# RWKV's output products in two groups of one shape (state, then u) instead of by turns

## The chip, the cores and the metric

One core of a Trainium2 chip runs the kernel. The metric is the device time of one execution in microseconds (us), the median of several; lower is better. TensorE (PE) does the products, VectorE (DVE) and ScalarE (ACT) take results out of the accumulation banks, GpSimd (POOL) works on SBUF alone, SyncE (SP) issues most DMAs.

## The reference

The reference is the trunk of a diffusion model: two layers over 256 context tokens and 256 latent tokens of 1024 features. Each layer has a token mixer of two halves of 512 features, RWKV-7 (eight heads of 64) and gated linear attention (GLA), then a feed-forward block (dense in layer 0, top-2 of 8 experts in layer 1). Both mixers run forwards and backwards over the tokens. The part that matters here is RWKV's recurrence:

```python
def step(s, inp):
    r_t, w_t, k_t, v_t, kk_t, a_t = inp
    s = (s * w_t[:, :, None, :]
         - jnp.einsum('bhvk,bhk->bhv', s, kk_t)[..., None] * (kk_t * a_t)[:, :, None, :]
         + v_t[..., None] * k_t[:, :, None, :])
    return s, jnp.einsum('bhvk,bhk->bhv', s, r_t)
```

Only the latent tokens' output is returned, so layer 1 needs RWKV's outputs of the context tokens only as a state.

## The kernel before, in words

**Chunks.** The recurrence is worked out in chunks of 64 tokens. A batch b (0 to 7) is one step of the chunked recurrence, for all eight heads and both directions at once: batches 0 to 3 are the context tokens, 4 to 7 the latent ones. Within a batch there are 8 places (d, p): direction d and pair of heads p. The even head of a pair lies on partitions 0 to 63 (`lo`), the odd one on 64 to 127 (`hi`).

**Lanes.** A batch passes through these generators: `rwkv_front` (lane F, L710) makes decays and scaled vectors; `rwkv_pairs` (P, L794) the triangular products between tokens, and sends the matrices that are to be inverted to DRAM (L820, L821); `rwkv_invert` (I, L837) loads their diagonal blocks back (L843) and inverts them on POOL (L848, L849); `rwkv_load` (L, L855) sends the result to DRAM (L862) and loads it as the tile Q (L864); `rwkv_mid` (M, L868) begins with DVE's transpose of Q into R (L896) and doubles the size of the blocks by products on PE (L884, L885); `rwkv_chain` (C, L946) does the recurrence: products with the old state (L961, L962), with the inverse (L970, L971), for the new state (L979, L980), and then the outputs y (L996 to L1012). `rwkv_post` (Z) and `rwkv_bonus` (B) finish the tokens; `ada` (A, L388) is independent work on the next modulation weights, put between as filler.

**Order.** The order in which the lanes take their steps is a string written out by hand for each layer, `RW_ORDER` (L52), played by `play` (L214). A step is what a generator does between two `yield`s. `may` (L1260) holds a step back only by counts of finished batches and steps. Each engine runs its instructions in the order in which they were issued, so the string fixes the order on every queue.

**The outputs.** For each place (d, p) the output is the sum of two products: the triangular matrix with u and the values (L1000: the weights u are 128 partitions by 64 columns, so all rows and half of the columns of the array), and the scaled vectors with the old state S (L1002: 64 partitions by 64 columns). The results of the even heads go to partitions 0 to 63 of one accumulation bank `a`, those of the odd heads to partitions 64 to 127 of another, `b_`. Float32 operands make two instructions of each product in the trace. One step does direction 0 (16 products, 32 instructions), the next direction 1, and the step after takes the sums out of both banks (L1005 to L1010). With S None (batch 0 of layer 0; layer 1's batch 0 makes no y) there is no product with the state. Layer 0 makes y for all eight batches, layer 1 for batches 4 to 7: 12 batches in all, 11 of them with both kinds of product.

Of the kernel before, what the change touches and what calls it, by code (L numbers as in the profile page):

```python
# [16 lines left out]
P = 128  # L17
# [14 lines left out]
# blocks of 128 columns of w_in in the order of use: rw r 0-3, k 4-7, v 8-11, w 12, a 13, g 14;  # L32
# gla q 0-1, k 2-3, v 4-7, o 8-11, a 12
ORDER = ([("gl", b) for b in (12, 2, 0, 4, 5, 3, 1, 6, 7, 8, 9, 10, 11)] +
         [("rw", b) for b in (14, 12, 13, 8, 9, 10, 11, 4, 0, 5, 1, 6, 2, 7, 3)])
# blocks after which the columns of GLA's q, k, v of a pair of heads, of its gate, and of RWKV's v are there
GLA_QKV, GLA_O, GLA_V = (5, 9), 13, 20
FGROUPS = [(0, 8), (8, 15), (15, 22)]
# weight pieces before the second layer's w_in
FFN_END = 24 + 8 + 14 + 4 + 22 + 24  # L40
SCRATCH = {"ogs": (P, 4, T), "vfirst": (P, 4, T), "rx": (P, 8, 256), "nsc": (2, 64, 1024), "tsc": (2, 64, 1024)}
# the order in which the lanes of a layer's projections with GLA, and of its RWKV, take their steps
# [23 lines left out]
# columns of the per-layer vectors  # L66
# [8 lines left out]
# columns of the per-layer small matrices  # L75
# [6 lines left out]
# columns of the constants  # L82
# [9 lines left out]
def constants():  # L92
# [7 lines left out]
    s = q % C  # L100
# [5 lines left out]
    # alpha comes at half its size  # L106
# [10 lines left out]
    # rows of the odd, and of the even, blocks of 16 of either half  # L117
# [5 lines left out]
def body(tc, nc, A):  # L123
# [19 lines left out]
    def banks(**bufs):  # L143
        """The eight banks divided anew."""
        if psum[0] is not None:
            psum[2].close()
        psum[2:] = [ExitStack()]
        psum[0] = psum[2].enter_context(tc.tile_pool(name=nm("pp"), bufs=1, space=PSUM))
        psum[1] = bufs
# [32 lines left out]
    def bc(ap, n):  # L182
        """[P, ..., a] seen as [P, ..., a, n]."""
        return bass.AP(tensor=ap.tensor, offset=ap.offset, ap=[*ap.ap, [0, n]])

    def bcm(ap, n):
        """[P, ...] seen as [P, n, ...]."""
        a = ap.ap
        return bass.AP(tensor=ap.tensor, offset=ap.offset, ap=[a[0], [0, n], *a[1:]])
# [5 lines left out]
    def steps(g, n):  # L195
        """n steps of g; whether it goes on."""
        for _ in range(n):
            if next(g, g) is g:
                return False
        return True  # L200
# [5 lines left out]
    def interleave(*gens, fill=None, rate=1):  # L206
        """A step of each in turn until all are through, and rate steps of fill beside them."""
# [6 lines left out]
    def play(lanes, order, may, extra={}):  # L214
        """Steps of the lanes (lists of generators, one after the other) in a given order; may(lane, done, step) tells
        whether a lane's next step may come. What is passed over or left is made in the end.
        extra: what a letter does that is no lane's."""
# [21 lines left out]
    # ------------------------------------------------------------ weight stream  # L239
    pieces = []  # L240

    class Stream:
# [23 lines left out]
        def room(self, n):  # L266
            """The pieces that there is room for when the first n are through."""
            return n + NR + (self.nx if self.more is not None else 0)

        def widen(self, p, n):  # L270
            """n more places for pieces, of pool p."""
# [4 lines left out]
        def split(self, upto):  # L276
            """Half pieces up to upto as two float32r parts."""
# [14 lines left out]
        def ahead(self, k, n):  # L292
            """Split half piece k and those up to n - 1 after it, as far as they are of a kind."""
# [16 lines left out]
        def half(self):  # L310
            """The next half piece; the one after it is split too, and more where there is room."""
# [3 lines left out]
        def get(self):  # L315
            """The next piece, both halves; the one after it is split too where there is room."""
# [26 lines left out]
    # the experts' chunks of 256 columns: 0, 1 the halves of gate and up, 2 down, which runs behind  # L343
# [12 lines left out]
    def dense_gen(out, hl, off, stride, xh, xl, ks, n0, n1):  # L356
        """out[128 features, tokens n0..n1] over the blocks ks of 128, in three float32r passes."""
# [11 lines left out]
    def dense_steps(out, w, xh, xl, n0, each):  # L369
        """out[128 features, tokens n0..] with one half piece, three products and a step at a time."""  # L370
# [8 lines left out]
    # ------------------------------------------------------------ modulation  # L379
# [8 lines left out]
    def ada(l, i0, i1, tag="acc"):  # L388
        """Columns 256 * i0.. of silu(c) @ ada_w + ada_b, features on partitions."""
# [29 lines left out]
    def staggered(gens, lag):  # L419
        """Each generator lag steps behind the one before."""  # L420
# [10 lines left out]
    class Squares:  # L431
        """Sums over the features of the squares of n columns."""
# [5 lines left out]
        def ready(self):  # L438
            """The table of Ln, before it is waited for."""
# [10 lines left out]
        def mm(self, keep=0):  # L450
            """The products of all but the last keep."""
# [4 lines left out]
        def r(self):  # L456
            """(mean + eps) ** -0.5, on all partitions."""
# [15 lines left out]
    def norm_mod(l, which, res, r, n0, hh, hl, tp, keep=None):  # L473
        """Modulation of res (tokens n0..) times r, as two float32r parts."""
# [20 lines left out]
        # every engine has a share  # L495
# [14 lines left out]
    def gated(l, which, dst, src, k, n0):  # L510
        """dst = src times the gate of feature block k, tokens n0.. (both hold these)."""
# [5 lines left out]
    def add_out(m, r, res, tp, nxt=None, dst=None):  # L517
        """dst = res + m r; the squares of the sums go to nxt."""
# [21 lines left out]
    # ------------------------------------------------------------ gated linear attention  # L540
    def gla_pair(l, n0, hp, M2, gab, q_, gk, gv, gad, og, tp, need):
        """Heads 2 hp and 2 hp + 1: their share of og becomes the mixer's output."""
# [81 lines left out]
        for n in range(0, 8, 2):  # L624
# [7 lines left out]
            # contributions to the state: chunks of even and odd place in different banks  # L632
# [53 lines left out]
    # ------------------------------------------------------------ RWKV-7  # L686
    # A batch b = 4 seg + i is the step i of a segment's recurrences: chunk i forwards, chunk 3 - i backwards, of all
    # eight heads. Tiles have [direction, pair of heads].
    NB = 16              # the blocks that are inverted row by row
# [3 lines left out]
    def image(t, b, q):  # L693
        """Block q of all matrices of batch b in DRAM: [head, direction, pair; NB rows; NB columns]."""
# [3 lines left out]
    def chunk(b, d):  # L698
        """The tokens of batch b in direction d."""
# [4 lines left out]
    def cut(t, b):  # L704
        """[.., tokens] as [direction, .., 64] of batch b."""
# [4 lines left out]
    def rwkv_front(l, b, X, tp):  # L710
        """Decays, and alpha, rho, beta, kappa scaled by them; the bonus."""
# [30 lines left out]
        # F: beta, kappa  # L742
# [36 lines left out]
    def rwkv_bonus(l, b, X, tp):  # L779
        """k_eff of both directions, r, r_k, summed over a head, times v."""  # L780
# [13 lines left out]
    def rwkv_pairs(l, b, X, tp):  # L794
        """The triangular products between tokens."""
        need_y = l == 0 or b >= 4
        arl, bk, Pt = X["scaled"].pop(b)
        # columns 0: with alpha, before t; 1: with rho, up to t. Rows of even heads: beta, kappa; of odd: kappa, beta
# [16 lines left out]
        # Nt: N transposed forwards, N backwards: above the diagonal either way  # L815
# [6 lines left out]
        # beta, kappa with tokens on partitions  # L822
# [14 lines left out]
    def rwkv_invert(b, X, tp):  # L837
        """A diagonal block to a lane: L = (I - N)^-1 forwards, its transpose backwards."""
# [16 lines left out]
    def rwkv_load(b, X, tp):  # L855
        """The inverted diagonal blocks come back."""
        # forwards (I - N)^-1 grows in Q and its transpose in R, backwards the other way round
# [10 lines left out]
    def rwkv_mid(l, b, X, tp):  # L868
        """(I - N)^-1 from its diagonal blocks, by doubling their size; values beside the places of u."""
# [4 lines left out]
        # values under (even heads) or over (odd) the places of u  # L874
# [17 lines left out]
        def alternate(x, d):       # the columns of every other block of 16  # L892
# [22 lines left out]
        # blocks of 16: their rows and columns lie by turns  # L915
# [20 lines left out]
        for d in range(2):  # L936
            # the transpose: above the diagonal forwards
# [8 lines left out]
    def rwkv_chain(l, b, X, tp):  # L946
        """A step of the recurrences, and its outputs."""
# [45 lines left out]
        if not need_y:  # L993
            yield True
            return
        a, b_ = ps("pc"), ps("pc")  # L996
        for d in range(2):
            for d_, p, o in mats[4 * d:4 * d + 4]:
                for t, h, u, A_ in ((a, lo, ux, AX), (b_, hi, uy, AY)):
                    mm(t[h, o], u[:, d, p, :], A_[:, d, p, 1, :], start=True, stop=S is None)  # L1000
                    if S is not None:
                        mm(t[h, o], S[h, d, p, :], arl[h, d, p, 1, :], start=False, stop=True)  # L1002
            yield
        y = cut(X["y"], b)
# [9 lines left out]
    def rwkv_post(l, b, X, tp):  # L1014
        """Head norm, bonus and gate of the tokens that are through with batch b."""
# [39 lines left out]
    def mixing(l, hctx):  # L1055
        """Token mixing of layer l; hands back its results (y of the heads, og) and their pools."""
# [47 lines left out]
        def conv_silu(pt, b, dst, s0):  # L1104
            """dst = 2 silu(conv(p)) over columns s0.."""
# [11 lines left out]
        def kk_norm(i):  # L1117
            """k k_k over its norm, halved."""
# [18 lines left out]
        def project(blocks):  # L1137
            """The blocks of h @ w_in that come next in the weight stream, a few products at a time."""
# [38 lines left out]
        def residual():  # L1177
            """v += (v of the first layer - v) * sigmoid(v0 + v @ v_down @ v_up)"""
# [43 lines left out]
        with pool("rw", "right") as tp:  # L1222
# [15 lines left out]
            def og_back():  # L1238
                """The other mixer's results come back, into the place of kk, which is through."""
# [20 lines left out]
            def may(n, done, step):  # L1260
                """What a step takes is there, and so is room for what it makes."""
# [21 lines left out]
            def warm(step):  # L1283
                """A product that nobody takes: the tensor engine's clock falls to half when it has had little to do."""
# [79 lines left out]
    def moe(l, res, r):  # L1364
# [12 lines left out]
        with pool("mh", "right") as hp:  # L1377
# [18 lines left out]
            # tokens on partitions  # L1396
# [10 lines left out]
            # the two greatest logits, the first of equals  # L1407
# [18 lines left out]
            # a token's place among those of its expert, and how many an expert has  # L1426
# [9 lines left out]
            # their weights  # L1436
# [23 lines left out]
        def choose(es, base, gt, g, w, tp, bufs):  # L1460
            """One-hot matrices of the slots base..base+127 of experts es: G tokens by slots, GT slots by tokens, w their
# [356 lines left out]
```

## Time and profile before

| what | value |
|---|---|
| time, median of 3 runs | 2515.29 us (2515.1 to 2521.45) |
| span of the profiled execution, first to last instruction | 2510.1 us |
| the median less that span | 5.2 us |
| PE busy | 2287.4 us, 91% of the span, 14765 matmuls |
| DVE busy | 1531.4 us, 61% |
| ACT busy | 1283.8 us, 51% |
| POOL busy | 248.0 us, 10% |
| mean granted TensorE clock | 0.917 |

The profiled execution's own time is not listed apart from its span; the 5.2 us between the median and the span are what lies around the instructions. The granted clock is 1.0 at 2.4 GHz and 0.5 at 1.2 GHz; a fraction between is a mean over a stretch. RWKV's stage of layer 0 runs from about 288 to 610 us of the span, that of layer 1 from about 1330 to 1605 us. A busy PE is not PE at its peak: matmuls overlap, so how fast products follow each other is read from their starts, not from their durations.

### The profile page before, as it was taken

To read this page: it belongs to the slowest core of one execution; us is meant where nothing else is said; L and a number is where in the kernel's file an instruction comes from. 1 tells how busy PE (TensorE), PEld (TensorE's weight loads), DVE (VectorE), ACT (ScalarE), POOL (GpSimd) and SP (SyncE) were. 2 spreads that over 40 slices of the span, in tenths; PEclk is the share of its full clock that TensorE was granted. 3 is DMA by queue.
4 is the path that set the end of the run, shared out by engine and by line. 5 is a ranking of instruction groups with operands and counts; after the bars stand their busy time and mean duration, and the time that the engine had idled before them with its cause. 6 is when DMAs were issued, how large, how long until landed. Compare 5 with 4: busy or idle time off the path is not lost. (4 is left out here: it accounts for less than half of the span.)

```text
span 2510.1 us, 37231 instructions
## 1 busy us (share of the span) xinstructions
PE 2287.4 (91%) x14765; PEld 1796.9 (72%) x14765; DVE 1531.4 (61%) x2236; ACT 1283.8 (51%) x1893; POOL 248.0 (10%) x597
## 2 busy tenths in 40 slices
PE   6999789998879999979997789869999999999997
PEld 3777577766658888847865667648787877877875
DVE  3647454623253233355674553358999898899996
ACT  3434443433342322354453442467777777777775
POOL 2000053320010000020002443000000000000000
PEclk8989888876979999988996988779999999999999
DMA  6211213452211313122222342248998998999992
GB/s 250 88 58 68 89 41 106 123 169 86 99 50 59 128 67 128 56 81 84 85 84 85 99 140 76 75 161 333 343 358 335 337 354 336 349 350 348 358 353 85
DMA packets 110310, 431.31 MB, mean 172 GB/s; under 512 B 51584, under 2 KB 54144, under 8 KB 61744
## 3 DMA queue, kind: packets, MB, share of 16 engines
q1 hardware_dynamic: 102800, 378.06, 41.9%
q10 hardware_dynamic: 5472, 39.85, 4.6%
q0 software_dynamic: 1856, 10.95, 1.2%
q8 instruction: 118, 1.93, 0.3%
q14 instruction: 64, 0.52, 0.1%
HBM read 418.33 MB, written 10.49 MB: 171 GB/s over the span
## 5 line engine op out<-in xcount | busy, mean ns | idle before, releaser
L289 DVE TENSOR_TENSOR lo<-raw,hi 128x1024 fp32r<-128x1024 f32 (+1 forms) x668 | 798.2, 1223 | 207.6 <-ACT hi L288 193.9
L288 ACT CAST hi<-raw 128x1024 fp32r<-128x1024 f32 (+1 forms) x668 | 685.2, 1048 | 156.0 <-PE ps_acc L1523 68.0
L1523 PE MATMUL ps_acc<-hi,gh 128*128 128x512 f32 x704 | 284.8, 405 | 0.0
L1523 PE MATMUL ps_acc<-hi,gl 128*128 128x512 f32 x704 | 278.3, 395 | 0.0
L1523 PE MATMUL ps_acc<-lo,gh 128*128 128x512 f32 x704 | 277.8, 395 | 0.0
L375 PE MATMUL ps_acc<-hh,hi 128*128 128x512 f32 (+1 forms) x448 | 180.5, 403 | 13.7 <-ACT hh L503 11.7
L375 PE MATMUL ps_acc<-hl,hi 128*128 128x512 f32 (+1 forms) x448 | 171.9, 384 | 2.9 <-POOL hl L507 2.1
L375 PE MATMUL ps_acc<-hh,lo 128*128 128x512 f32 (+1 forms) x448 | 171.5, 383 | 1.5 <-DVE lo L289 1.5
L1523 PEld LDWEIGHTS ps_acc<-lo,gh 128*128 128x128 f32 x704 | 132.1, 188 | 32.3 <-DVE lo L289 0.2
L1523 PEld LDWEIGHTS ps_acc<-hi,gl 128*128 128x128 f32 x704 | 132.4, 188 | 27.2
L1523 PEld LDWEIGHTS ps_acc<-hi,gh 128*128 128x128 f32 x704 | 132.2, 188 | 27.4
L1547 PE MATMUL ps_pc<-hi,eah 128*128 128x512 f32 x352 | 139.5, 396 | 0.0
L1547 PE MATMUL ps_pc<-lo,eah 128*128 128x512 f32 x352 | 139.0, 395 | 0.0
L1547 PE MATMUL ps_pc<-hi,eal 128*128 128x512 f32 x352 | 139.0, 395 | 0.0
L375 PEld LDWEIGHTS ps_acc<-hh,hi 128*128 128x128 f32 x448 | 88.4, 197 | 37.8 <-ACT hh L503 6.3
L375 PEld LDWEIGHTS ps_acc<-hl,hi 128*128 128x128 f32 x448 | 88.4, 197 | 19.8 <-POOL hl L507 3.6
L375 PEld LDWEIGHTS ps_acc<-hh,lo 128*128 128x128 f32 x448 | 88.3, 197 | 18.6 <-DVE lo L289 2.8
L1337 DVE TENSOR_TENSOR s<-s,ps_pa 128x512 f32<-128x512 f32 x22 | 15.1, 688 | 140.9 <-PE ps_pa L363 140.9
L848 POOL TENSOR_TENSOR Tt<-Nl,Tl 64x15 f32<-64x15 f32 (+7 forms) x240 | 71.9, 300 | 159.3 <-DMA Nl<-nsc 142.4
L396 PE MATMUL ps_acc<-raw,silc 128*32 128x256 f32 x768 | 66.2, 452 | 23.0 <-DMA raw<-ada 12.6
L533 POOL TENSOR_TENSOR xn<-macc,rstd 128x256 f32<-128x256 f32 x2 | 1.8, 925 | 842.7 <-ACT rstd L461 842.7
L453 PE MATMUL ps_pc<-nsq,ones 128*128 128x512 f32 (+1 forms) x112 | 57.3, 637 | 30.2 <-ACT nsq L447 30.1
(410 smaller groups left out, 4649.0 us busy)
## 6 DMA issues: line engine op xcount, KB each, us to landing
raw<-moe SPq DMA_DIRECT2D x264, 1024.0 KB, 6.1
raw<-ada ACTq DMA_DIRECT2D x34, 1024.0 KB, 5.3
raw<-win SPq DMA_DIRECT2D x28, 1024.0 KB, 4.9
raw<-fgu SPq DMA_DIRECT2D x22, 1024.0 KB, 4.8
raw<-ada SPq DMA_DIRECT2D x14, 1024.0 KB, 5.0
raw<-fdn SPq DMA_DIRECT2D x16, 448.0 KB, 3.2
res<-xc POOLq DMA_DIRECT2D x2, 2048.0 KB, 12.8
Q<-tsc SPq DMA_DIRECT2D x32, 128.0 KB, 2.8
```

The lines of the kernel that those rows point to most:

```text
L288: sc.copy(hi[:, :n], t[:, a * HALF:a * HALF + n])
L289: ve.tensor_tensor(lo[:, :n], t[:, a * HALF:a * HALF + n], hi[:, :n], ALU.subtract)
L375: mm(out, a[:, o], x[:, k, n0:T], start=(k == 0 and j == 0), stop=(k == KB - 1 and j == 2))
L396: mm(pt[32 * q:32 * q + 32, :256], silc[:, k, :], raw[:, k * 256:k * 256 + 256], start=(kk == 0), stop=(kk == 1), tile_position=(0, 32 * q))
L453: mm(self.pt, ones, self.todo.pop(0)[:, :self.n], start=(self.made == 0), stop=(self.made == KB - 1))
L533: e.tensor_tensor(t, m[:, k, :], r, ALU.mult)
L848: gp.tensor_tensor(tmp[:, u, j], bc(Nl[:, s, t], s + 1), bcm(Tl[:, s, j], NB - 1 - s), ALU.mult)
L1337: ve.tensor_tensor(s, s, pu, ALU.mult)
L1523: mm(pg, x[:, k, :], ww, start=(k == 0 and j == 0), stop=(k == 7 and j == 2))
L1547: mm(pd[q], x[:, i * P:i * P + P], ww, start=(c == 0 and i == 0 and j == 0), stop=(c == 10 and i == 1 and j == 2))
```

## The change

The 32 products of a batch's outputs are the same. They are issued as all 16 products with the state, a step boundary, all 16 products with u, a step boundary. The number of steps stays. The opening flag (`start`), which before stood on each product with u, stands on the first product in each bank alone; the products with u then add to what lies there. With S None the first of the two steps is empty, and the second has all 16 products with u. The rest of the diff takes comments away without moving a line; behind L1003 the lines move down by seven.

```diff
         a, b_ = ps("pc"), ps("pc")
-        for d in range(2):
-            for d_, p, o in mats[4 * d:4 * d + 4]:
-                for t, h, u, A_ in ((a, lo, ux, AX), (b_, hi, uy, AY)):
-                    mm(t[h, o], u[:, d, p, :], A_[:, d, p, 1, :], start=True, stop=S is None)
-                    if S is not None:
-                        mm(t[h, o], S[h, d, p, :], arl[h, d, p, 1, :], start=False, stop=True)
-            yield
+        if S is None:
+            yield
+        else:
+            for n, (d, p, o) in enumerate(mats):
+                for t, h in ((a, lo), (b_, hi)):
+                    mm(t[h, o], S[h, d, p, :], arl[h, d, p, 1, :], start=(n == 0), stop=False, skip_group_check=True)
+            yield
+        for n, (d, p, o) in enumerate(mats):
+            for t, h, u, A_ in ((a, lo, ux, AX), (b_, hi, uy, AY)):
+                mm(t[h, o], u[:, d, p, :], A_[:, d, p, 1, :], start=(S is None and n == 0), stop=True,
+                   skip_group_check=True)
+        yield
```

## Rows read from the trace of the kernel before

**Rows 1.** The page: busy time of all engines, and the clock in 40 slices.

```profile
PE 2287.4 (91%) x14765; PEld 1796.9 (72%) x14765; DVE 1531.4 (61%) x2236; ACT 1283.8 (51%) x1893; POOL 248.0 (10%) x597
...
PEclk8989888876979999988996988779999999999999
```

**Rows 2.** Busy time in a stretch of layer 0's RWKV: us, engines, clock, DMA share, GB/s.

```profile
400.00:450.00 50.00, 49.49 (x652) 36.95 (x652) 26.62 (x55) 22.00 (x47) 13.72 (x38) 0.87 0.30 86
```

**Rows 3.** PE's waits, 345 to 600 us: us in total, times, longest.

```profile
PE ps_pc L980 <- DVE uy L974: 2.9, 1, 2.9
...
PE ps_acc L404 <- ACT arow L400: 0.7, 2, 0.5
```

**Rows 4.** Lines 1000 and 1002: matmuls, ns min/median/max, first and last start, form.

```profile
L1000 PE MATMUL ps_pc<-AX,ux x192: 222/270/370, 358.1 to 1591.5; 128*64 128x64 f32 x192
...
L1002 PE MATMUL ps_pc<-arl,S x352: 218/267/367, 391.9 to 1592.8; 64*64 64x64 f32 x176
```

**Rows 5.** Timeline of PE in the first output step of batch 1, layer 0: start, us.

```profile
391.62 0.33 PE L1000 MATMUL ps_pc<-AX,ux 128*64 128x64 f32 x2
391.88 0.33 PE L1002 MATMUL ps_pc<-arl,S 64*64 64x64 f32 x2
```

**Rows 6.** The 17 stretches of output steps with both kinds: us, PE busy, clock, DMA.

```profile
391.62:395.73 4.11, 4.11 (x34) 0.99 0.16 34
396.74:403.19 6.45, 6.45 (x36) 0.50 0.30 104
424.39:428.49 4.10, 4.10 (x33) 1.00 0.25 43
429.97:434.52 4.55, 4.55 (x35) 0.86 0.70 236
...
535.06:539.22 4.16, 4.16 (x33) 0.98 0.82 321
541.09:547.31 6.22, 6.22 (x38) 0.50 0.07 8
...
1540.31:1549.59 9.28, 9.28 (x65) 0.81 0.22 54
...
sum 111.71, PE 111.71; mean PE 6.57
```

**Rows 7.** Groups of one shape: L970/L971; L1000 of batch 0; L884/L885. Columns of rows 2.

```profile
376.67:377.75 1.08, 1.08 (x34) 1.01 (x33) 0.00 (x0) 0.00 (x0) 0.00 (x0) 1.00 0.06 23
...
359.13:360.27 1.14, 1.14 (x30) 1.00 (x30) 1.13 (x2) 0.06 (x1) 0.98 (x3) 1.00 0.00 0
...
385.18:387.08 1.90, 1.90 (x33) 1.78 (x32) 1.86 (x5) 0.00 (x0) 0.00 (x0) 0.50 0.20 17
```

**Rows 8.** Nine stretches at half clock that hold output steps. Columns of rows 2.

```profile
sum 92.30, PE 92.30 PEld 64.79 DVE 14.20 ACT 15.98 POOL 33.75; mean PE 10.26 PEld 7.20 DVE 1.58 ACT 1.78 POOL 3.75
```

**Rows 9.** Timeline: the inverse's load and DVE's transpose of it; line 864's landing times.

```profile
404.06 1.11 SPq L864 DMA_DIRECT2D Q<-tsc  x2
...
411.34 0.71 DVE L896 STREAM_TRANSPOSE R<-Q 128x512 f32<-128x512 f32 x1
...
445.26 1.11 SPq L864 DMA_DIRECT2D Q<-tsc  x2
...
449.52 0.71 DVE L896 STREAM_TRANSPOSE R<-Q 128x512 f32<-128x512 f32 x1
...
548.19 1.73 SPq L864 DMA_DIRECT2D Q<-tsc  x2
...
553.84 0.70 DVE L896 STREAM_TRANSPOSE R<-Q 128x512 f32<-128x512 f32 x1
...
1546.28 1.11 SPq L864 DMA_DIRECT2D Q<-tsc  x2
...
1554.24 0.71 DVE L896 STREAM_TRANSPOSE R<-Q 128x512 f32<-128x512 f32 x1
...
DMA to landing us min/median/max: 2.5/2.8/5.9
```

## The prediction

> **What bounds the kernel now.** I read the busy times first: PE is busy 91% of the span, no other engine above 61%, and the granted clock dips in RWKV's two stages (slices 5 to 9 and 21 to 26 of 40) [rows 1]. Then the stretches inside layer 0's stage: PE is busy 49.5 us of 50, DVE about half of that, POOL a quarter [rows 2], and the longest single wait of PE between 345 and 600 us is 2.9 us [rows 3]. So PE's queue sets the pace there, and the fillers of the hand-written order keep it full. But busy is not well used. The two output lines have matmuls of 218 to 370 ns [rows 4], as all small products here do; what counts is how fast they follow each other. By turns, two instructions of one shape start 0.26 us before two of the other [rows 5]: about 0.13 us an instruction. Thus 32 instructions take 4.1 us at the full clock and 6.45 us at half clock [rows 6]. The same shapes in a group of their own follow each other four times as fast: the 32 instructions of 64 by 64 on lines 970 and 971, whose halves, weights and banks lie just as those of the state's products, take 1.08 us; 30 of u's own, which stood alone in batch 0 because there is no state yet, take 1.14 us; and at half clock such a group of 32 takes 1.90 us [rows 7]. So it is the change of shape from one product to the next that costs, not the work.
>
> **What the change removes.** Layer 0 has 7 batches with both kinds, layer 1 has 4: 11 batches of 64 instructions, 704 (192 for each bank on line 1000 less batch 0's 32 in all, and 352 on line 1002 [rows 4]). They take 111.7 us of PE now, all of it busy [rows 6], 10.15 us a batch. After: 22 groups. At 1.08 us each that is 24 us, at 1.90 us it is 42; I take 25, most groups at the full clock, since the half clock came in the middle of the slow blocks. **Removed: 87 us, between 70 and 88.**
>
> **The clock.** In nine stretches of together 92.3 us the clock was at half and output steps lie in them or just before [rows 8]. From lengths and clocks of the 17 output stretches [rows 6] some 44 us of the 92 are output products, counted above. The other 48 us would run up to twice as fast at the full clock, if it no longer fell: 0 to 24 us. No row shows what the clock does once the slow blocks are gone, and waits may make it fall in other places, so I take the middle: **12 us**.
>
> **What is moved, and what it is moved past.** The products with the state come ahead of those with u. They read the state of the batch before and scaled vectors made long ago, and need nothing that is late; they now run before the wait for u that PE met at times, at no cost. No DMA, no POOL and no SP instruction stands in these steps, so no queue but PE's is reordered. In batch 0 the first step becomes empty and 16 products go into the next; they run at the price of rows 7 either way, and PE waited for its next work behind them: nothing. One opening flag in place of 16 a bank is a bit on the same instructions: no row shows such a group, the nearest row is the second product of each pair, which adds to the bank now at the same pace as the first [rows 5], so I take nothing, and 0.1 us a group either way at most.
>
> **What is late next.** PE reaches what follows a block about 8 us earlier; whatever did not start from that block is then waited for. The long chain that runs beside the blocks is the inversion: matrices to DRAM, POOL's 30 instructions, back to DRAM, Q loaded, and DVE's transpose of Q, behind which DVE's other work queues for the chain lane, and PE behind that. I estimate the arrival as the second load's issue plus the median landing of 2.8 us. In layer 0 batch 3's Q is there at about 407.4 and taken at 411.3 (3.9 us to spare); batch 4's at 448.6 and 449.5 (0.9); batch 7's at 551.9 and 553.8 (1.9); layer 1's batch 7's at 1549.6 and 1554.2 (4.6) [rows 9]. The output blocks that run on PE in between lose 10.6 - 2.3 = 8.3, 6.3, 8.1 and 7.0 us [rows 6, 7]. Waits of 4.4, 5.4, 6.2 and 2.4 us come up: **18 us given back**. Three more places have 6 us and more to spare and I count nothing. Below, 0: PE's first product with R comes some us after the transpose, and other steps lie between. Above, 40: the three other places, and what the clock gave.
> Second, a slow step of 4 to 6 us covered the copies by ACT and DVE between two products of the mid and chain lanes; a group of 1.1 us covers less. The nearest row is PE's wait for a copy by ACT, up to 0.5 us [rows 3]. At 22 groups: **11 us given back**, 0 to 22.
> DVE and ACT, which waited at the head of their queues for the outputs, get that time free; neither was the bound [rows 2], so nothing.
>
> **Sum.** 87 + 12 - 18 - 11 = 70 us less. Everything behind the two stages starts that much earlier, and nothing in it waits for a fixed time. The profiled span of 2510.1 becomes 2440; it stands 5.2 us below the median of the runs, so the time becomes **2445 us**.
>
> **Rivals.**
> *The inversion becomes the bound.* Then all that is saved ahead of a later inversion comes back as waits at line 896, and only the last two batches' outputs of either stage keep it: four of 10.15 - 2.3 us, 31 us, 2484 us. For it: batch 4's 0.9 us to spare. Against it: the other places, and that PE has other batches' work before R is needed. Chance 0.12.
> *u's group stays slow.* A group of products with 128 rows might not load weights beside running products. Then it keeps the pace of rows 5: 4.1 us, so 11 x (1.1 + 4.1) = 57 us, 55 removed; clock 6 and waits 18 shrink alike: 43 us less, 2472 us. Against it stand the 1.14 us of batch 0 [rows 7], the very line. Chance 0.03.
> The Trainium skill, TensorE: Matmul & The Clock Gate (section Part 3: Packing small matmuls — row/col tiling), says that a weight load overlaps running matmuls only when their row groups differ, and all of u's products use the same rows. By that rule the time would be this rival's; the trace of batch 0 disagrees.
> *Slower, by the clock.* PE's place is line 884 behind the transposes: a wait there lets the clock fall over the densest products. The 2.9 us wait [rows 3] stands just ahead of the half-clock group of 1.90 us [rows 7]. The price is double time for array work. With 87 us gone and 29 of waits added, it decides from 66 us of extra time on, which is 66 us of work now at full clock falling to half; at 80 us the time is 2537 us. Seven waits, each with some 7 us of half clock, cost only half of 49. Chance 0.03.
> *No change.* The order on PE is not what sets the pace of the products and all come out as now: 2515 us. Rows 7 speak against it. Chance 0.02.
> *All of it.* No waits, the clock stays: 111 us less, 2404 us. Chance 0.05.
> The forecast keeps 0.75, with 2412 to 2475 of its own.
>
> **Numbers.** A measurement of this kernel can tell about 0.3%, 7.5 us, from no change. Faster: 0.75 + 0.12 + 0.03 + 0.05 = 0.95; the same 0.02; slower 0.03. The range goes from 2412, short of the last rival, up to 2485, which takes in the inversion.
>
> **What would show it.** Right: the 32 products with the state and then with u in about 1.1 us each; the sum of output blocks near 25 us; DVE's waits for outputs on lines 1009 and 1010 (as numbered before) cut to about a us; new idle time at line 896 for Q of batches 3, 4 and 7; most of the nine half-clock stretches gone. Wrong: groups of 2 us or more at the full clock; a PE that idles over 60 us more in the two stages; or half-clock stretches that sum up to more than now.

## The result, and the profile after

The changed kernel takes **2443.3 us**, the median of four runs (2437.1 to 2448.6). The kernel before, beside it on the same chip, takes 2515.2. The ratio is **0.971, with an interval of 0.9683 to 0.9737**: 72 us less. The profiled execution took 2443.0 us and its span is 2441.2, so only 1.8 us lie around the instructions.

The page of the changed kernel: its span, busy times, and PE and its clock in 40 slices.

```profile
span 2441.2 us, 37232 instructions
...
PE 2188.5 (90%) x14765; PEld 1733.9 (71%) x14765; DVE 1530.8 (63%) x2236; ACT 1283.7 (53%) x1893; POOL 245.0 (10%) x597
...
PE   6999788878699999969978887779999999999997
...
PEclk8989888988899999979996989789999999999999
```

Against [rows 1] the same 14765 matmuls keep PE busy for 98.9 us less (2287.4 to 2188.5). The span fell by only 68.9. So PE's idle time, span less busy time, rose from 222.7 to 252.7 us: **30 us were given back as idle time**. The busy times of DVE and ACT stand still, as they should when only PE's order changes. Now the 22 groups. The windows of PE over them, from the first start to the end of the last instruction (columns: us, PE busy with its instructions, clock, DMA share, GB/s):

```profile
390.96:392.11 1.15, 1.15 (x37) 1.00 0.00 0
392.61:393.76 1.15, 1.15 (x40) 1.00 0.06 14
...
424.00:425.86 1.86, 1.86 (x37) 0.57 0.46 79
...
1488.53:1490.24 1.71, 1.35 (x40) 1.00 0.00 0
...
sum 27.02, PE 26.50; mean PE 1.20
```

The first two lines are batch 1 of layer 0, state and then u. In [rows 6] the same 64 instructions took 4.11 and 6.45 us. All 22 groups keep PE busy for 26.5 us in place of 111.7. (The stretches of [rows 6] stop a little short of the last instruction's end; taken to that end, as here, they are 113.9 us.) One group alone still runs mostly at half clock (424.00, clock 0.57); on two of them a wait of a few tenths of a us lies inside.

Where the other time went is seen in the two stages as wholes, from the first product of `rwkv_front` to the first instruction of the work behind. First the kernel before, then the changed one (the same columns):

```profile
288.70:622.10 333.40, 307.16 (x3581) 0.80 0.31 97
1329.80:1606.10 276.30, 236.96 (x3080) 0.82 0.29 83
sum 609.70, PE 544.12; mean PE 272.06
```

```profile
288.00:576.50 288.50, 241.29 (x3581) 0.88 0.36 112
1284.20:1537.80 253.60, 204.46 (x3080) 0.85 0.31 91
sum 542.10, PE 445.75; mean PE 222.87
```

The stages are 44.9 and 22.7 us shorter, 67.6 of the span's 68.9; what lies between and behind them is as long as before. In them PE's busy time fell by 98.4 us and its idle time rose from 65.6 to 96.4. Since the clock is either 1.0 or 0.5, a mean of 0.80 says that 40% of a stage ran at half clock. That makes 233 us before (333.4 x 0.40 + 276.3 x 0.36) and 145 after.

Who waits now? What ends the idle time of DVE ahead of its transpose of Q (line 896), and ahead of taking the outputs (line 1009 before, 1016 after), first in the kernel before, then in the changed one (us in total, times):

```profile
  DMA Q<-tsc: 31.8, 6
...
  PE ps_pc L1002: 35.2, 6
```

```profile
  DMA Q<-tsc: 74.5, 14
...
  PE ps_pc L1008: 1.2, 2
```

DVE stands 9 us longer than it did (75.7 in place of 67.0), and nearly all of it for a load. PE's waits in layer 0's stage and then in layer 1's (us in total, times, longest):

```profile
PE ps_pf L718 <- DMA up<-up: 13.1, 1, 13.1
PE ps_acc L1050 <- DVE mods L406: 9.2, 2, 8.1
...
PE ps_pc L971 <- DVE Rs L966: 3.3, 2, 2.9
...
PE ps_acc L396 <- DVE mods L406: 2.1, 4, 1.0
...
PE ps_pb L884 <- DMA Q<-tsc: 7.4, 2, 6.0
```

The first is the stage's start, where PE waited 12 to 13 us for a load before the change too. The second doesn't name Q at all. The timeline of the changed kernel around it, in layer 0's batch 7, shows why (start, us, engine, line, in brackets the idle time before it and what ended it):

```profile
530.71 1.11 SPq L864 DMA_DIRECT2D Q<-tsc  x2
...
534.02 0.71 DVE L896 STREAM_TRANSPOSE R<-Q 128x512 f32<-128x512 f32 x1 [13.44 <-DMA Q<-tsc]
534.65 0.38 DVE L966 COPY Rs<-ps_pc 128x256 f32<-128x256 f32 x1
534.96 0.14 DVE L406 TENSOR_TENSOR mods<-ps_acc,vec 128x4 f32<-128x4 f32 x1
...
535.16 1.12 PE L1050 MATMUL ps_acc<-wag,gup 128*128 128x64 f32 x4 [8.14 <-DVE mods L406]
```

DVE stood 13.4 us at the head of its queue for Q. Behind the transpose stood a copy for the chain and a small addition of the filler, which frees the bank that PE wanted. PE waited 8.1 us for an addition of 0.14 us that had nothing to do with Q. In batch 3 the 2.9 us have the same root (line 966 follows line 896), and in batch 4 the 1.0 us (line 406 comes behind it); in layer 1's batch 7 PE waits for Q itself, 6.0 us. Not every wait behind this transpose is new. PE stood behind it before the change too, 2.9 us in layer 0's batch 2 and 6.7 us in layer 1's batch 5, and it stands there as long now (3.1 and 6.7 us).

### The profile page after: what moved, and what is told of

Same layout as the page of the kernel before. It is cut to its first block, busy times and chain, and to the rows that moved or that the text cites. A ratio compares the mean times of both kernels' runs of the same rounds, so it can differ in the third digit from the quotient of the medians.

```text
span 2441.2 us, 37232 instructions
## 1 busy us (share of the span) xinstructions
PE 2188.5 (90%) x14765; PEld 1733.9 (71%) x14765; DVE 1530.8 (63%) x2236; ACT 1283.7 (53%) x1893; POOL 245.0 (10%) x597
## 5 line engine op out<-in xcount | busy, mean ns | idle before, releaser
L848 POOL TENSOR_TENSOR Tt<-Nl,Tl 64x15 f32<-64x15 f32 (+7 forms) x240 | 71.3, 297 | 146.8 <-DMA Nl<-nsc 129.9
```

Of the source, the lines that this page charges most:

```text
L848: gp.tensor_tensor(tmp[:, u, j], bc(Nl[:, s, t], s + 1), bcm(Tl[:, s, j], NB - 1 - s), ALU.mult)
```

## The experiments

**What makes the turns slow.** Four runs change the product loops alone; each diff is against the changed kernel, whose two loops ("if S is None" to the second step's end) these lines replace.

```diff
+        for d in range(2):
+            for n in range(4):
+                (d1, p1, o1), (d2, p2, o2) = mats[4 * d + n], mats[4 - 4 * d + n]
+                for t, h, u, A_ in ((a, lo, ux, AX), (b_, hi, uy, AY)):
+                    mm(t[h, o1], u[:, d1, p1, :], A_[:, d1, p1, 1, :], start=(d == 0 and n == 0), stop=True,
+                       skip_group_check=True)
+                    if S is not None:
+                        mm(t[h, o2], S[h, d2, p2, :], arl[h, d2, p2, 1, :], start=False, stop=True, skip_group_check=True)
             yield
```

> The shapes come by turns as before the change (u, state, u, state), but the product with the state that follows one with u goes to another place of the bank (the other direction's), and each bank is opened once. Theory (a change of shape from one product to the next costs): 32 instructions take 4.1 us at the full clock as before, the 11 batches some 100 to 112 us, time near 2515 us. Rival (a product that adds to the very columns that the one before it wrote has to wait for that one): 32 instructions take 1.1 us, the 11 batches 25 to 30 us, time near 2443 us.

2517.5 us in one run, with 2518.2 for the kernel before. The windows of the first two output steps (us, PE busy, clock, DMA share, GB/s):

```profile
391.11:395.21 4.10, 4.10 (x33) 1.00 0.16 30
396.02:402.48 6.46, 6.46 (x36) 0.50 0.31 117
```

The second product of a pair now goes to the columns of the other direction, and the pace is that of [rows 6] within a hundredth of a us. That it was slow because it adds to columns still being written is ruled out. The opposite run leaves the products with the state out and makes those with u twice on the same columns, so that there is one shape:

```diff
+                for t, h, u, A_ in ((a, lo, ux, AX), (b_, hi, uy, AY)):
+                    mm(t[h, o], u[:, d, p, :], A_[:, d, p, 1, :], start=True, stop=S is None)
+                    if S is not None:
+                        mm(t[h, o], u[:, d, p, :], A_[:, d, p, 1, :], start=False, stop=True)
```

> As before the change, but each product with the state is left out, and the product with u is made a second time in its place, at once and into the same columns: one shape throughout, and each second product adds to what the one before it wrote. Theory (change of shape): 1.1 us for 32 instructions, the 11 batches about 25 us, time near 2445 us. Rival (adding to the same columns waits): 4.1 us for 32, some 100 to 112 us, time near 2515 us.

2442.7 us in one run. The window of a step, from the first start to the end of the last of its 32 instructions:

```profile
390.20:391.40 1.20, 1.20 (x40) 1.00 0.00 0
```

In the changed kernel a group of 32 takes 1.15 us, measured alike. So adding at once to the columns of the instruction before costs next to nothing, and neither do the openings that this loop sets for each product. The two runs together leave the change of shape. The third asks whether it is paid per change or per product, and changes shape half as often:

```diff
+                if S is not None:
+                    for t, h in ((a, lo), (b_, hi)):
+                        mm(t[h, o], S[h, d, p, :], arl[h, d, p, 1, :], start=(d == 0 and p == 0), stop=False,
+                           skip_group_check=True)
+                for t, h, u, A_ in ((a, lo, ux, AX), (b_, hi, uy, AY)):
+                    mm(t[h, o], u[:, d, p, :], A_[:, d, p, 1, :], start=(S is None and d == 0 and p == 0), stop=True,
+                       skip_group_check=True)
```

> At each place the two products with the state (even and odd head), then the two with u: a change of shape every second product in place of every one. Theory (each change has its own price, (4.11 - 1.08) / 16 = 0.19 us): 32 instructions with 8 changes take 1.1 + 1.5 = 2.6 us at the full clock, the 11 batches 57 to 65 us, time near 2475 us. Rival (what counts is whether even and odd head of one shape run beside each other): each such pair of products then runs at the pace of a group, 1.1 to 1.3 us for 32 instructions, time near 2445 us.

2465.0 us in one run. The window of the first of these steps, and the timeline of PE in it:

```profile
390.16:392.27 2.11, 2.11 (x34) 1.00 0.03 12
```

```profile
390.16 0.33 PE L1003 MATMUL ps_pc<-arl,S 64*64 64x64 f32 x4
390.42 0.27 PE L1006 MATMUL ps_pc<-AX,ux 128*64 128x64 f32 x1
390.43 0.27 PE L1006 MATMUL ps_pc<-AY,uy 128*64 128x64 f32 x1
...
390.69 0.33 PE L1003 MATMUL ps_pc<-arl,S 64*64 64x64 f32 x4
```

2.1 us for 32 instructions, faster than expected. By turns a run of one shape is two instructions and takes 0.26 us ([rows 5]: 391.62 to 391.88); here a run is four instructions and takes 0.26 or 0.27 us too (390.16, 390.42, 390.69). So the cost is no fixed sum on top of the work: a run of one shape takes about 0.26 us at the full clock, with two instructions or with four. Sixteen such runs are the 4.1 us of the kernel before, eight are the 2.1 us here. The shortest records of one matmul are 0.22 us [rows 4]. That fits a next shape which starts only when the products of the last are through; the records of PE's ends are modelled, so this reading is the likely one and not proved.
The Trainium skill, TensorEngine Tiling (Array Packing), section Key Properties, says that a change of tiling mode drains the engine. The runs agree with it, at 0.26 us a run of products.

One more case was open: whether two products of different shape are slow also where they meet in no column and no bank. Here the product with the state that follows one with u is of the other head. The change back to u stays in one half.

```diff
+                for (t, h, u, A_), (t2, h2) in (((a, lo, ux, AX), (b_, hi)), ((b_, hi, uy, AY), (a, lo))):
+                    mm(t[h, o1], u[:, d1, p1, :], A_[:, d1, p1, 1, :], start=(S is None and d == 0 and n == 0 or h == lo and d == 0 and n == 0),
+                       stop=True, skip_group_check=True)
+                    if S is not None:
+                        mm(t2[h2, o2], S[h2, d2, p2, :], arl[h2, d2, p2, 1, :], start=(h2 == hi and d == 0 and n == 0),
+                           stop=True, skip_group_check=True)
```

> Shapes by turns once more, but the product with the state that follows one with u is of the other head: it writes the other half of the array's columns and the other bank, at another place. Theory (any change of shape waits until the running products have ended): 32 instructions take 4.1 us at the full clock, the 11 batches 100 to 115 us, time near 2515 us. Rival (the second product waits only because its weights go to columns in which the first still runs): 1.1 to 2.1 us for 32 instructions, time 2443 to 2465 us.

2513.7 us in one run, with 2512.4 for the kernel before. The timeline of PE:

```profile
390.96 0.33 PE L1003 MATMUL ps_pc<-AX,ux 128*64 128x64 f32 x2
391.22 0.32 PE L1006 MATMUL ps_pc<-arl,S 64*64 64x64 f32 x2
391.48 0.33 PE L1003 MATMUL ps_pc<-AY,uy 128*64 128x64 f32 x2
```

0.26 us from change to change again, across the halves and within one: disjoint columns and banks don't help. The products with u use all 128 rows, so the two shapes always share rows; no run parts these.

**What the change gave back.** The theory is the inversion's chain (matrices to DRAM, POOL, DRAM, Q) and DVE's queue behind line 896. The most direct test makes the chain short in both kernels. Beside them the changed kernel runs once more as it is:

> The changed kernel as it is, for comparison on the same chip with the runs beside it: 2443 us, 0.971 of the time before.

2442.5 us, ratio 0.9708 (0.9674 to 0.9742); the kernel before takes 2516.7 here. The edit of the other two leaves out 13 of the inversion's 15 steps:

```diff
-            gp.tensor_tensor(tmp[:, u, j], bc(Nl[:, s, t], s + 1), bcm(Tl[:, s, j], NB - 1 - s), ALU.mult)
-            gp.tensor_tensor(Tl[:, t, j], Tl[:, t, j], tmp[:, u, j], ALU.add)
+            if s < 2:
+                gp.tensor_tensor(tmp[:, u, j], bc(Nl[:, s, t], s + 1), bcm(Tl[:, s, j], NB - 1 - s), ALU.mult)
+                gp.tensor_tensor(Tl[:, t, j], Tl[:, t, j], tmp[:, u, j], ALU.add)
```

> The changed kernel with 13 of the 15 steps of the inversion on POOL left out (the inverse is wrong then), some 9 us of POOL's 11 to 12 us per batch; loads, stores and all else stay. Theory (of the 29 us that the change gave back, some 18 are waits for the inversion): PE's waits behind line 896 vanish, and the time falls by 12 to 20 us against the changed kernel, 2423 to 2431 us. Rival (the waits come from other chains that the slow products had covered): it falls by less than 5 us.

> The kernel before with the same 13 steps of the inversion left out. Theory (the inversion was hidden under the slow products): the time falls by no more than 2 to 7 us, of which most is PE's two waits of 3.9 us for the load of the inverse; 2508 to 2513 us. Rival (the inversion cost as much before the change as after): it falls by as much as the changed kernel does, 12 us or more.

Changed kernel with 2 of 15 steps: 2395.2 us, ratio 0.9522 (0.9489 to 0.9556). Kernel before with 2 of 15: 2497.5 us, ratio 0.9931 (0.9904 to 0.9958). Both sizes were missed. The length of the inversion costs the kernel before 19 us (2516.7 less 2497.5) and the changed one 47 (2442.5 less 2395.2). Without it, the change is worth 102 us in place of 74, so some 28 us were given back to the inversion; the intervals leave about 14 either way. The windows of the two stages tell idle time from slow time, first the kernel before with the short inversion, then the changed one:

```profile
288.70:627.00 338.30, 312.07 (x3581) 0.79 0.31 96
1332.70:1591.40 258.70, 230.53 (x3080) 0.84 0.31 89
sum 597.00, PE 542.60; mean PE 271.30
```

```profile
288.20:549.80 261.60, 232.70 (x3581) 0.90 0.40 124
1257.70:1489.40 231.70, 198.39 (x3080) 0.88 0.34 99
sum 493.30, PE 431.09; mean PE 215.54
```

With the short inversion the change takes 111.5 us of busy time away (542.6 to 431.1) and adds only 7.8 of idle (54.4 to 62.2). With the full one it takes 98.4 and adds 30.8. By these four profiled executions the inversion's length takes back 23 us as idle PE, and 13 us as longer busy time, at a lower clock in the changed kernel (0.88 and 0.85, against 0.90 and 0.88 with the short inversion). Together that is 36 us, where the medians say 28, within their 14 either way. That the waits are what lowers the clock fits, and no run shows it apart. The 7.8 that stay are waits of another kind. In both of these kernels DVE waits less than 15 us in all for Q ahead of the transpose; in the changed kernel above it was 74.5.

**Can it be had back?** First by an order that queues less behind line 896: the transpose goes two steps down, just ahead of the first product that reads R.

```diff
-        ve.transpose(R.rearrange(f4), Q.rearrange(f4))
-        yield
         vt = ps("pb"), ps("pb")
...
+        yield
+        ve.transpose(R.rearrange(f4), Q.rearrange(f4))
         yield
         a, b_ = prod(*nt, *halves(Q, R))
```

> The changed kernel, with one step of the mid lane moved: DVE's transpose of the loaded inverse comes two steps later, just ahead of the first product that reads it, and no longer holds up what is queued behind it on DVE. Theory (the new idle time of PE, about 18 us, comes from DVE's queue standing at this transpose): PE's idle time in layer 0's RWKV falls by 3 to 8 us, most of it the wait of 8.1 us behind batch 7's transpose, time 2433 to 2441 us. Rival (PE itself needs the inverse, or the idle time is of other waits): PE's idle time and the time stay, 2441 to 2447 us, or it gets slower by the 0.7 us of a transpose that now stands right ahead of its reader, 16 times: 2450 us.

2437.2 us, ratio 0.9687 (0.9671 to 0.9703). What ended DVE's idle time ahead of the moved line:

```profile
  DMA Q<-tsc: 45.7, 11
```

DVE waits 45.7 us in place of 74.5, as the theory has it. In the profiled run PE's idle time in the two stages is 85.8 us (530.8 less 445.0), 10.6 under the changed kernel's. PE's waits on line 1050 fell from 9.2 to 1.8 us, the one of 8.1 us among them, but its waits for ACT's copy on line 404 grew from 6.9 to 13.5. That run, 2429.7 us, is the lowest of the four. The median is 6 us lower, but its interval overlaps that of the change, so no gain is shown.

Then by moving the inversion from POOL to DVE:

```diff
+        yield
...
-            gp.tensor_tensor(tmp[:, u, j], bc(Nl[:, s, t], s + 1), bcm(Tl[:, s, j], NB - 1 - s), ALU.mult)
-            gp.tensor_tensor(Tl[:, t, j], Tl[:, t, j], tmp[:, u, j], ALU.add)
-            if s % 4 == 3:
+            ve.tensor_tensor(tmp[:, u, j], bc(Nl[:, s, t], s + 1), bcm(Tl[:, s, j], NB - 1 - s), ALU.mult)
+            ve.tensor_tensor(Tl[:, t, j], Tl[:, t, j], tmp[:, u, j], ALU.add)
+            if s in (4, 9):
```

> The changed kernel with the 30 instructions of the inversion on DVE in place of POOL, and their steps cut so that the load comes in the first and five rounds in each of the other three. Theory (the inversion's length is what PE waits for, and DVE, busy for half of RWKV's stages, has room): an inversion of 3 to 6 us in place of 11, time 2425 to 2438 us. Rival (DVE's queue now stands at the load of the matrices, 3 to 5 us a batch, and PE behind it): 2445 to 2480 us.

2510.3 us, ratio 0.9965 (0.9944 to 0.9987): nearly the whole gain lost, worse than the rival had it. Its two stages, and DVE's idle time ahead of the inversion's first line for the matrices, and ahead of the transpose for Q (us in total, times):

```profile
287.50:617.50 330.00, 256.95 (x3581) 0.83 0.32 98
1324.80:1605.00 280.20, 219.34 (x3080) 0.79 0.28 82
sum 610.20, PE 476.29; mean PE 238.14
```

```profile
  DMA Nl<-nsc: 13.5, 5
...
  DMA Q<-tsc: 34.2, 9
```

PE idles 133.9 us, 37.6 more than after the change, and runs at a lower clock in both stages. In the changed kernel POOL stood 129.9 us at these loads, and little else was queued behind it. On DVE such a wait stands in the queue on which PE's next operands are made. DVE waits less for Q than in the changed kernel (34.2 in place of 74.5), but it now stands 13.5 us at the load of the matrices, and it has 95 us more work in the two stages (384 in place of 289). PE's waits that DVE ended rose from 64 to 109 us there. Which of the two costs more, the standing or the work, is not shown apart.

Then by taking the steps of the lanes F, P, I and L up to 8, and up to 16, letters earlier than the hand-written order (with the transpose of the run above):

```diff
-        for n in order:
-            if n in extra:
-                extra[n](step)
+        left = list(order)
+        while left:
+            for i, n in enumerate(left[:8 if "I" in lanes else 0]):
+                if n in "FPIL" and one(n):
+                    left.pop(i)
+                    break
             else:
-                one(n)
+                n = left.pop(0)
...
```

> The kernel with the late transpose, and the steps of the lanes F, P, I and L (front, pairs, inversion, load) taken up to 8 letters of the hand-written order earlier where the rules of that order let them. Theory (what is left of PE's idle time in RWKV's stages is mostly the inversion's length, so an earlier start of it is worth up to the 47 us that the short inversion gave): 10 to 25 us below the late transpose, 2412 to 2427 us. Rival (the earlier steps stand in the way of the chain's on PE and DVE, or the rules leave them no room): 2430 to 2450 us.

> The same with up to 16 letters. Theory: as good as 8 earlier or better by up to 10 us, since an inversion takes 25 to 30 us and 16 letters are about that much of PE's work. Rival: worse than 8 earlier by 5 us or more, since fillers are all left to the end, where PE then waits for the chain's short products.

2486.5 us, ratio 0.9905 (0.9873 to 0.9938), and 2477.4 us, ratio 0.9865 (0.9828 to 0.9901). The first is outside what both its theory and its rival had; the second is 9 us better than the first, as its theory had it. Both are slower than the change. In the run with 8 letters, DVE's wait for Q and the page's busy times:

```profile
  DMA Q<-tsc: 6.3, 3
...
PE 2222.1 (89%) x14765; PEld 1756.0 (71%) x14765; DVE 1529.2 (62%) x2236; ACT 1284.2 (52%) x1893; POOL 242.4 (10%) x597
```

The wait for Q did all but vanish, 6.3 us in place of 74.5. But PE's busy time is 33.6 us longer with the same 14765 matmuls, at a mean clock of 0.917 against 0.933, and its idle time is 10 us longer (2484.9 less 2222.1, against 252.7). With 16 letters DVE doesn't wait for Q at all, and the time is still 34 us above the change. So the wait for Q can be removed by order, but this order pays more elsewhere, most of it in slower work. That PE's short dependent steps now follow each other too closely is likely, and not shown.

Last, filler, together with the later transpose: three pieces of it at the head of each stage, before the first step of lane F, which waits there for a load.

```diff
-            play(lanes, RW_ORDER[l], may, dict(D=warm))
+            order = RW_ORDER[l]
+            play(lanes, "A" * 15 + order.replace("A", "", 15), may, dict(D=warm))
```

> The kernel with the late transpose, and the first three of the filler pieces of each layer's RWKV made ahead of everything else in that stage, where PE stands 13 and 12 us for a load. Theory (fillers are worth more where PE waits for a load than among the slow chains, where 1.1 to 1.7 us of PE's time each leave a PE that is still mostly busy): 3 to 10 us below the late transpose, 2427 to 2434 us. Rival (the places that they leave are now limited by the inversion, so that the stage gets no shorter, or the first step is put off by them): 2435 to 2445 us.

2447.4 us, ratio 0.9727 (0.9701 to 0.9752): missed. The window in which the filler ran, and the stage's first product:

```profile
280.00:294.00 14.00, 8.70 (x60) 0.52 0.75 266
```

```profile
294.07 1.97 PE L718 MATMUL ps_pf<-up,wag 128*64 128x512 f32 x4
```

The fillers ran at a clock of 0.52, and the first product came at 294.1 in place of 288.0. The filler itself began only at 283.1, after PE had waited 7.0 us for line 1100, and then took 11 us. The 13 us that PE waits there in the changed kernel were not all free: filler that ends behind the gap puts the chain off, here by 6 us. How much of the 10 us against the later transpose alone this explains is not shown. No version was shown to beat the change.

## Why the prediction was right

It said 2445 us and 70 us less; 2443.3 and 72 were measured. By its own steps:

**Removed: 87 us, held.** The sums of the output stretches, each to the end of its last instruction: the kernel before, then the kernel before and the changed one with the short inversion.

```profile
sum 113.85, PE 113.85; mean PE 6.70
```

```profile
sum 118.10, PE 118.10; mean PE 6.95
```

```profile
sum 26.69, PE 26.68; mean PE 1.40
```

113.9 less 26.5 is 87.4; it had put the groups at 25. The prices of rows 7 carried over from other lines: 1.08 us a group, 1.15 with the last instruction's tail. e1, e2, e3 and e9 show its reason, that the change of shape costs and not the work, and e3 gives it a better form.

**The clock: 12 us, held, but as a balance.** The busy time fell by 98.4 us, 11 more than the products. With the short inversion it falls by 111.5, and the products by 91.4 (118.1 less 26.7), so 20 us are left, not far below the upper bound of 24. The waits that came up took about half of it away again. The prediction took the middle for want of a row. That the middle came out is in part luck: two effects met there.

**What is late next: 18 us at line 896; the mechanism held, the size was somewhat small.** The mechanism is shown: the short inversion takes the waits away, and with them 23 us of idle PE, 5 more than forecast. The four places were right, their sizes were not: 2.9, 1.0, 8.1 and 6.0 us of PE's time in batches 3, 4 and 7 of layer 0 and batch 7 of layer 1, 18.0 in all, where 4.4, 5.4, 6.2 and 2.4 stood. That these four sum up to 18 is luck; their errors cancel. The room to spare was worked out with the median landing, while the trace of the kernel before has batch 4's load landing at 449.43 and that of layer 1's batch 7 at 1550.77: 0.1 and 3.5 us to spare in place of 0.9 and 4.6. In layer 0's batches 3, 4 and 7 the price was set by what stood behind the transpose in DVE's queue.

**Copies: 11 us, not confirmed as such.** 7.8 us of idle time stay when the inversion is short. But PE's waits for ACT and DVE in the mid and chain lanes, where the prediction put them, grow by only 1.4 us there (12.9 to 14.3); most of the rest stands in the filler and the lanes P and Z. So this term was too big where the one before was too small. Idle time in all was forecast at 29 us and came out at 30.8, with errors that cancel.

**What was wrong in the sum's frame** is small: the span was said to stand 5.2 us below the time, as if all of that lay around it. The runs of the changed kernel show 1.8 us around a span; the other 3.4 were the difference between the profiled run and the median.

**The rivals.** *u's group stays slow* falls by the trace: 32 instructions with all 128 rows take 1.15 us (392.61 to 393.76). The Trainium skill, TensorE: Matmul & The Clock Gate (section Part 3: Packing small matmuls — row/col tiling), says that a weight load overlaps running matmuls only when their row groups differ. By that rule the time would have been this rival's, 2472 us; the 1.15 us decide against it here. *The inversion becomes the bound* came true in part: the inversion takes back 28 of 102 us, where that rival had it take most. *All of it* (111 us) comes near where the inversion is short: 102 us. *Slower by the clock* needed 66 us of work falling to half clock; the time at half clock fell instead, from 233 to 145 us.

What stays open: whether a later transpose is worth its 6 us, which of PE's waits lets the clock fall, and what in PE makes a change of shape take 0.26 us.

## What to carry to other kernels

Look at how far apart products start, not at how long they last. If the shape changes between neighbours, group them by shape; a group of the same shape elsewhere in the trace gives the price beforehand. Then ask which load or copy the slow products were hiding, and what else is queued behind the instruction that will now stand waiting for it: here that gave back about a quarter of the gain (28 of 102 us, give or take 14).

## What was not expected of the hardware

- A run of one shape takes 0.26 us whether it has two instructions or four (e3), and also where the two shapes share no column and no bank (e9). In a group of 32 an instruction costs 0.03 us.
- Two products in a row onto the same columns run about as fast as onto different ones: 1.20 us for 32 (e2), against 1.15.
- The waits came with more than their length: 23 us of idle PE from the inversion stood beside 13 us of longer busy time at a lower granted clock (e6 and e7, one profiled execution each).
